# Attention in a hybrid trunk: the two key heads of a head tile issued as a pair on TensorE

## The chip, the cores and the metric

The kernel runs on one core of one Trainium2 chip. The metric is the device time of one execution in microseconds (us), the median of several runs.

## What is computed

Two trunk layers over 256 latent tokens, with 256 context tokens that go through the same weights, width 1024, in fp32. Each layer has a token mixer of three parallel groups (attention, RWKV-7 scan, Hyena long convolution), an output projection, and a channel mixer: a dense SwiGLU in layer 0, a SwiGLU over 8 experts in layer 1. The attention group has 8 query heads of 64 and 2 key heads; latent queries read latent and context keys, context queries read context keys alone:

```python
def gqa_attend(q, k, v):
    s = jnp.einsum('bqgrd,bkgd->bgrqk', q, k, ...) * (HEAD_DIM ** -0.5)
    p = jax.nn.softmax(s, axis=-1).astype(v.dtype)
    return jnp.einsum('bgrqk,bkgd->bqgrd', p, v)
# in each layer, beside the RWKV and Hyena groups:
k_all = jnp.concatenate([kl, kc], 1)    # latent queries: 512 keys
out_lat = gqa_attend(ql, k_all, v_all)
out_ctx = gqa_attend(qc, kc, vc)        # context queries: 256 keys; layer 0 alone
o = jnp.concatenate([att, rwkv, hyena], -1) @ w_out
```

## The kernel before

The program is written in parts (input projection, preparation of the scan, scan, attention, Hyena, output projection, channel mixer), each for one layer and one stream (LAT, CTX). A tile scheduler fixes the order on each engine when the kernel is built: it takes the instruction that is ready by its own estimate, with the program's order as priority. Each engine then works its list off in that order, so an instruction that waits holds up everything behind it on its engine.

`attend` is called three times: for the context tokens of layer 0 (at about 222 to 290 us of the profiled execution), for the latent tokens of layer 0 (about 345 to 461 us) and for those of layer 1 (about 1150 to 1281 us). Other parts lie between its instructions: the RWKV scan, whose states `rS` follow each other as a chain and whose outputs are `rY`, the scan's readout (`ryT`, `rg`), and projections (`u`). A stretch of an attend after the scan's last `rY` is called a tail below: 433 to 461 us and 1239 to 1281 us.

An attend runs over 4 head tiles. A head tile is 128 partitions: head i of key head 0 on partitions 0 to 63, head i of key head 1 on 64 to 127. The queries stand in two tiles of 128 (`qt`). One step is one key head and one query tile, so there are 4 steps in a head tile and 16 in an attend. A step does these: scores `aS` (64 contraction rows, so half of the array's rows; 512 keys, or 256 for the context) on TensorE into one of two PSUM banks of tag "a"; the row maximum and its scaling on VectorE; exp with its sum on ScalarE, giving P (`aP`); transposes of P's 128x128 blocks on TensorE into the only PSUM bank of tag "t" (`aPT`); one copy of that bank by ScalarE into SBUF; and the outputs `ao` (64 output columns, half of the array's columns, 128 queries to a matmul) into a bank of tag "g". After 4 steps `azb` spreads the reciprocal sums over the partitions (through tag "t" too), and two VectorE and ScalarE steps write the head tile's result into `oTa`, which the output projection reads. The loads of that projection's weights go into buffers (`wraw`) that are taken in turn.

```python
BANKS = {"g": 3, "w0": 1, "w1": 1, "a": 2, "t": 1}
```

In a trace a matmul of fp32 data stands as two records, so `x2` there is one score matmul and `x4` two outputs.

Of the kernel before, what the change touches and what calls it, by code (L numbers as in the profile page):

```python
# [15 lines left out]
def feature_tiles():  # L16
    """Columns of w_in per 128-wide tile, -1 for padding."""
# [45 lines left out]
NLAST = 512  # of the first group, kept throughout  # L63
# [8 lines left out]
def constants():  # L72
# [11 lines left out]
    # x -> (-x1, x0) on pairs: out[m] = sum_k perm[k, m] x[k]  # L84
# [14 lines left out]
    ang = np.concatenate([row[:, None] * inv, col[:, None] * inv], -1).astype(np.float64)  # [L, 32]  # L99
# [6 lines left out]
    S = np.sin(th)  # [t, k]  # L106
    S[:, 0] = (-1.0) ** k  # column k = 0 holds the Nyquist term
    put("C", C.reshape(2, 128, 256).transpose(1, 0, 2))
    # forward: lhsT [t, k]; inverse: lhsT [k, t] -> S transposed
# [17 lines left out]
    a, b = (p % 32)[:, None], np.arange(32)[None]  # row s, column t  # L127
    # per direction: (A, B, -A, B) masks; A strict, B inclusive
# [3 lines left out]
    # token order: ltri[p, tt, q] = 1 where token tt*128+p precedes q within the tile  # L132
# [5 lines left out]
    # within a chunk, from its first (second) half to the other one  # L138
# [5 lines left out]
def layout(i):  # L144
    """Device arrays from the inputs: layout only."""
# [9 lines left out]
    aw = g("ada_w").reshape(2, 8, 128, 3, 4, 2, 256)  # l, k, p, r, j, h, n  # L155
    A["adaw"] = np.ascontiguousarray(aw.transpose(0, 3, 5, 1, 2, 4, 6))  # l, r, h, k, p, j, n
# [12 lines left out]
    A["win"] = np.ascontiguousarray(wp.reshape(2, 8, 128, 20, 128).transpose(0, 3, 2, 1, 4))  # l, tile, p, k, 128  # L169
    wo = g("w_out")[:, mix_rows()]  # L170
    A["wout"] = np.ascontiguousarray(wo.reshape(2, 4, 2, 128, 2, 512).transpose(0, 4, 1, 3, 2, 5))  # l, half, kh, p, k, n

    def w13(w1, w3):  # [..., 1024, 2816] -> [..., 11, kh, p, k, (w1 256 | w3 256)]
        e = w1.shape[0]
        u = np.stack([w1, w3], 1).reshape(e, 2, 4, 2, 128, 11, 256)  # e, m, kh, k, p, b, n
        return np.ascontiguousarray(u.transpose(0, 5, 2, 4, 3, 1, 6)).reshape(e, 11, 4, 128, 2, 512)

    def w2(w):  # [e, 2816, 1024] -> [e, half, 22, p, 512]
        e = w.shape[0]
        u = w.reshape(e, 11, 2, 128, 2, 512)  # L180
        return np.ascontiguousarray(u.transpose(0, 4, 1, 3, 2, 5))  # e, half, 11, p, 2, 512
# [6 lines left out]
    A["rows"] = np.stack([g("ln1_g"), g("ln1_b"), g("ln2_g"), g("ln2_b")], 1)  # l, 4, 1024  # L188
    pr = np.zeros((2, 128, NPRM), np.float32)

    def pp(name, a, col=0, r0=0):  # a: [2, rows]
        pr[:, r0:r0 + a.shape[1], PRM[name] + col] = a

    mu = g("rwkv_mu")  # [2, 2, 864]
# [64 lines left out]
class Trunk:  # L259
# [4 lines left out]
    def lasting(s, n):  # L264
        """n words per partition that are kept throughout."""
# [4 lines left out]
    def k(s, shape, name, dt=F32):  # L270
        """A tile. All of the pool's are of 4 KB per partition: up to 1 (2) KB, four (two) of a name share
        one; up to 512 bytes, the slots of a small lasting ring are used in turn."""
# [24 lines left out]
    def fresh(s, *names):  # L297
        """The next small tiles of these names do not share one with the past ones."""
        for n in names:
            s.packs.pop((n, s.w), None)  # L300
# [12 lines left out]
    def split(s, src, hi, lo, eng="a"):  # L313
        """hi + lo == src; both fit a float32r pass exactly."""
# [3 lines left out]
    def mm3(s, out, a, b, start, stop, **kw):  # L318
        """out += a.T @ b from (hi, lo) pairs: three float32r passes."""
# [5 lines left out]
    def rsqrt(s, x, n, eps, name):  # L325
        """x[:, :n] -> 1 / sqrt(x + eps): an estimate from the exponent, then Newton steps to float32."""
# [10 lines left out]
    def raw(s, src):  # L337
        """The next 4 KB per partition of the weight stream."""
# [4 lines left out]
        if s.w == "m" and s.loads % 16 == 0:  # some through another queue  # L343
# [1400 lines left out]
```

## Time and profile before

| | |
|---|---|
| time, median of 3 runs | 2166.26 us (2155.64 to 2171.59) |
| span of the profiled execution | 2151.5 us |
| TensorE (PE) busy | 2061.4 us (96%) |
| VectorE (DVE) busy | 1650.1 us (77%) |
| ScalarE (ACT) busy | 1117.6 us (52%) |

The profile comes from one execution; its span lies 14.8 us below the median and 4.1 us below the fastest run shown. PE is the matmul stream and PEld the loading of its weights, which overlaps it. PEclk is the clock that TensorE was granted, as a share of full speed.

### The profile page before, as it was taken

The page shows a single profiled execution, that of the slowest core. Times are in us where ns is not written, and L with a number is a line of the kernel's source. Part 1 is how long each engine was busy: PE and PEld are TensorE (multiplying, and loading weights), DVE is VectorE, ACT ScalarE, POOL GpSimd, SP SyncE. Part 2 cuts the span into 40 slices and gives each one's busy share as a digit, 9 for nine tenths or more (in the row PEclk, how much of TensorE's full clock was granted, in tenths as well). Part 3 has the DMA queues.
Part 4 walks back from the last instruction along what each step waited for, and adds up shares of the span by engine and source line. Part 5 has one row for each costly group of instructions (what it writes and reads, how often), then busy time and mean ns, then how long its engine had stood idle before and what let it go on. Part 6 is the DMA issues. An engine that isn't in the chain of part 4 may idle for free. (4 is left out here: it accounts for less than half of the span.)

```text
span 2151.5 us, 35770 instructions
## 1 busy us (share of the span) xinstructions
PE 2061.4 (96%) x13674; PEld 1684.2 (78%) x13674; DVE 1650.1 (77%) x3026; ACT 1117.6 (52%) x1639; POOL 111.3 (5%) x87
## 2 busy tenths in 40 slices
PE   8999999999999999989798998999999999999996
PEld 2878777678878898887487777788888888888885
DVE  6897777459754685776887448799899989998997
ACT  3532544242332344443244232787787877778773
POOL 0012001100000000010111100000000000000000
PEclk9999999999999999999899978899999999999998
DMA  8522332336686545323211018699999999999992
GB/s 292 191 74 98 138 129 90 114 115 230 247 335 244 196 177 196 138 88 113 104 60 33 31 56 335 218 319 362 363 334 368 354 344 350 361 358 345 360 356 107
DMA packets 147852, 469.15 MB, mean 218 GB/s; under 512 B 31636, under 2 KB 33972, under 8 KB 147672
## 3 DMA queue, kind: packets, MB, share of 16 engines
q1 hardware_dynamic: 123512, 446.27, 56.8%
q0 software_dynamic: 4816, 17.36, 2.2%
q10 hardware_dynamic: 19344, 3.15, 0.8%
q8 instruction: 109, 1.79, 0.3%
q14 instruction: 71, 0.58, 0.1%
HBM read 464.56 MB, written 2.16 MB: 217 GB/s over the span
## 5 line engine op out<-in xcount | busy, mean ns | idle before, releaser
L316 DVE TENSOR_TENSOR wlo<-wraw,whi 128x1024 fp32r<-128x1024 f32 x748 | 888.0, 1222 | 96.2 <-ACT whi L315 61.7
L315 ACT CAST whi<-wraw 128x1024 fp32r<-128x1024 f32 x748 | 751.7, 1049 | 143.6 <-DMA wraw<-in_fw_dram 40.6
L321 PE MATMUL ab<-whi,m_x 128*128 128x512 f32 x704 | 281.6, 400 | 0.0
L323 PE MATMUL ab<-whi,m_x 128*128 128x512 f32 x704 | 275.6, 391 | 0.0
L322 PE MATMUL ab<-wlo,m_x 128*128 128x512 f32 x704 | 275.0, 391 | 0.0
L321 PE MATMUL ab<-hp,whi 128*128 128x256 f32 x704 | 204.8, 292 | 2.6 <-ACT hp L315 2.0
L323 PE MATMUL ab<-hp,wlo 128*128 128x256 f32 x704 | 201.7, 287 | 1.8 <-DVE wlo L316 1.8
L322 PE MATMUL ab<-hp,whi 128*128 128x256 f32 x704 | 201.7, 287 | 1.3 <-DVE hp L316 1.1
L323 PEld LDWEIGHTS ab<-whi,m_x 128*128 128x128 f32 x704 | 132.1, 188 | 28.3
L321 PE MATMUL u<-hp,whi 128*128 128x256 f32 x512 | 150.2, 297 | 4.1 <-ACT hp L315 3.0
L322 PEld LDWEIGHTS ab<-wlo,m_x 128*128 128x128 f32 x704 | 132.5, 188 | 25.5 <-DVE wlo L316 0.2
L321 PEld LDWEIGHTS ab<-whi,m_x 128*128 128x128 f32 x704 | 132.2, 188 | 25.1
L321 PEld LDWEIGHTS ab<-hp,whi 128*128 128x128 f32 x704 | 135.9, 194 | 18.3 <-issue 11.0
L323 PE MATMUL u<-hp,wlo 128*128 128x256 f32 x512 | 147.9, 291 | 1.2 <-DVE wlo L316 1.1
L322 PE MATMUL u<-hp,whi 128*128 128x256 f32 x512 | 148.1, 292 | 0.0
L323 PEld LDWEIGHTS ab<-hp,wlo 128*128 128x128 f32 x704 | 136.1, 194 | 5.3 <-DVE wlo L316 2.9
L322 PEld LDWEIGHTS ab<-hp,whi 128*128 128x128 f32 x704 | 136.5, 194 | 2.1 <-DVE hp L316 2.0
L321 PE MATMUL mo<-whi,ffg 128*128 128x512 f32 x352 | 137.8, 392 | 0.0
L323 PE MATMUL mo<-whi,ffg 128*128 128x512 f32 x352 | 137.1, 390 | 0.0
L322 PE MATMUL mo<-wlo,ffg 128*128 128x512 f32 x352 | 137.0, 389 | 0.0
L957 POOL TENSOR_TENSOR rBD<-rAT,cst 128x1024 f32<-128x1024 f32 x28 | 67.5, 2418 | 932.8 <-DVE rTm L995 509.9
L321 PEld LDWEIGHTS u<-hp,whi 128*128 128x128 f32 x512 | 98.4, 194 | 15.9 <-issue 6.5
(395 smaller groups left out, 3610.3 us busy)
## 6 DMA issues: line engine op xcount, KB each, us to landing
wraw<-in_mw_dram SPq DMA_DIRECT2D x495, 512.0 KB, 5.6
wraw<-in_fw_dram SPq DMA_DIRECT2D x132, 512.0 KB, 5.2
wraw<-in_adaw_dram SPq DMA_DIRECT2D x96, 512.0 KB, 5.1
wraw<-in_win_dram SPq DMA_DIRECT2D x64, 512.0 KB, 5.7
wraw<-in_mw_dram POOLq DMA_DIRECT2D x33, 512.0 KB, 6.8
wraw<-in_wout_dram SPq DMA_DIRECT2D x24, 512.0 KB, 3.6
lngb<-in_rows_dram SPq DMA_DIRECT2D x12, 512.0 KB, 6.3
x<-in_xs_dram SPq DMA_DIRECT2D x8, 512.0 KB, 6.0
```

Of the source, the lines that this page charges most:

```text
L315: i = (s.nc.scalar.copy if eng == "a" else s.nc.vector.tensor_copy)(hi, src)
L316: return i, s.nc.vector.tensor_sub(lo, src, hi.bitcast(F32))
L321: mm(out, a[0], b[0], start=start, stop=False, **kw)
L322: mm(out, a[0], b[1], start=False, stop=False, **kw)
L323: mm(out, a[1], b[0], start=False, stop=stop, **kw)
L957: i = nc.gpsimd.tensor_mul(x.rearrange("p u (j t) -> p u j t", j=4), bc(ATu[:, :, m, None, :], [128, 8, 4, 32]), bc(mask.rearrange("p (j t ...
```

## The change

A step becomes one query tile with both key heads, so there are 2 steps in a head tile. Both score matmuls are issued one behind the other, ahead of other work that is ready, on rows 0 to 63 and 64 to 127 of the array and into both "a" banks; the first of them is put behind the last exp of the step before. The two transposed blocks go through the one "t" bank in turn, and the second is copied out by VectorE instead of ScalarE. The copies are kept for both query tiles, and the outputs come once in a head tile, at its end: for each block of keys one matmul for each key head, on columns 0 to 63 and 64 to 127, with all 256 queries. Each attend has 8 such steps. Line numbers behind this function are 12 higher in the changed kernel. The rest of the diff takes comments out and is not shown.

```diff
     def attend(s, l, g, oT):
         nc = s.nc
+        mm = nc.tensor.matmul
         ns = 2 if g["st"] == LAT else 1
-        nk = 256 * ns
+        nk, n = 256 * ns, 2 * ns
         q, qrs = g["q"], g["qrs"]
         keys = s.akv[l][:, 0, :ns].rearrange("p a b -> p (a b)")
         vals = s.akv[l][:, 1, :ns].rearrange("p a b -> p (a b)")
+        half, read = [slice(0, 64), slice(64, 128)], None
         for i in range(4):
-            op = s.bank("g", "ao")
+            T = [s.k([128, n, 256], "aPT") for _ in range(2)]
             zs = s.k([128, 2, 2], "az")
-            for g in range(2):
-                r0 = 64 * g
-                for qt in range(2):
-                    S = s.bank("a", "aS")[:, :nk]
-                    nc.tensor.matmul(S, q[r0:r0 + 64, i, 128 * qt:128 * qt + 128], keys[r0:r0 + 64, :], start=True,
-                                     stop=True)
-                    rs = qrs[i][:, 2 * qt + g:2 * qt + g + 1]
+            for qt in range(2):
+                qs = slice(128 * qt, 128 * qt + 128)
+                S = [s.bank("a", "aS")[:, :nk] for _ in range(2)]
+                with s.tc.high_priority():
+                    for h in range(2):
+                        m = mm(S[h], q[half[h], i, qs], keys[half[h], :], start=True, stop=True)
+                        if h == 0 and read is not None:
+                            s.order(m, read)
+                P = []
+                for h in range(2):
+                    rs = qrs[i][:, 2 * qt + h:2 * qt + h + 1]
                     m = s.k([128, 1], "am")
-                    nc.vector.tensor_reduce(m, S, axis=AX.X, op=OP.max)
+                    nc.vector.tensor_reduce(m, S[h], axis=AX.X, op=OP.max)
                     nc.vector.tensor_scalar(m, m, rs, -1.0, op0=OP.mult, op1=OP.mult)
-                    P = s.k([128, nk], "aP")
-                    nc.scalar.activation(P, S, AF.Exp, bias=m, scale=rs, accum_out=zs[:, qt, g:g + 1])
-                    pt = s.bank("t", "aPT")[:, :nk]
-                    for k in range(nk // 128):
-                        nc.tensor.transpose(pt[:, 128 * k:128 * k + 128], P[:, 128 * k:128 * k + 128], s.c("ident"))
-                    T = s.k([128, nk], "aPT")
-                    nc.scalar.copy(T, pt)
-                    for k in range(nk // 128):
-                        nc.tensor.matmul(op[r0:r0 + 64, 128 * qt:128 * qt + 128], vals[:, 128 * k + r0:128 * k + r0 + 64],
-                                         T[:, 128 * k:128 * k + 128], start=k == 0, stop=k == nk // 128 - 1)
-                    yield
+                    P.append(s.k([128, nk], "aP"))
+                    read = nc.scalar.activation(P[h], S[h], AF.Exp, bias=m, scale=rs, accum_out=zs[:, qt, h:h + 1])
+                for h in range(2):
+                    pt = s.bank("t", "aPT")[:, :nk].rearrange("p (k q) -> p k q", k=n)
+                    for k in range(n):
+                        nc.tensor.transpose(pt[:, k, :], P[h][:, 128 * k:128 * k + 128], s.c("ident"))
+                    done = (nc.scalar.copy if h == 0 else nc.vector.tensor_copy)(T[h][:, :, qs], pt)
+                yield
+            op = s.bank("g", "ao")[:, :256]
+            with s.tc.high_priority():
+                for k in range(n):
+                    for h in range(2):
+                        m = mm(op[half[h], :], vals[:, 128 * k + 64 * h:128 * k + 64 * h + 64], T[h][:, k, :],
+                               start=k == 0, stop=k == n - 1)
+                        if h == k == 0:
+                            s.order(m, done)
             nc.vector.reciprocal(zs, zs)
             b = s.bank("t", "azb")[:, :256]
             for qt in range(2):
                 s.spread(b[:, 128 * qt:128 * qt + 128], zs[:, qt])
             f, zb = s.k([128, 256], "mx"), s.k([128, 256], "mx")
             nc.scalar.copy(zb, b)
-            nc.vector.tensor_mul(f, op[:, :256], zb)
+            nc.vector.tensor_mul(f, op, zb)
             s.split(f, *oT[i])
         s.fresh("mx", "aP", "aPT")
```

TensorE's list in the tail of layer 1's attend before, where `aS` is scores, `aPT` transposes, `ao` outputs, `azb` the spread sums and `ryT` the scan's readout (a row's x4 counts equal instructions in a row):

```order
L770 MATMUL aS<-akv,aq 128x512 x2
L784 MATMUL ao<-aPT,akv 64x128 x4
L780 MATMUL aPT<-keep,aP 128x128 x4
L784 MATMUL ao<-aPT,akv 64x128 x4
L702 MATMUL azb<-keep 64x128 x4
L770 MATMUL aS<-akv,aq 128x512
L1181 MATMUL ryT<-keep,rvt 128x128 x4
L780 MATMUL aPT<-keep,aP 128x128 x4
L770 MATMUL aS<-akv,aq 128x512
```

and in the same tail after the change, where `Xc` and `Xs` belong to the Hyena part:

```order
L788 MATMUL aPT<-keep,aP 128x128 x4
L774 MATMUL aS<-akv,aq 128x512 x2
L788 MATMUL aPT<-keep,aP 128x128 x8
L795 MATMUL ao<-aPT,akv 64x256 x2
L774 MATMUL aS<-akv,aq 128x512 x2
L795 MATMUL ao<-aPT,akv 64x256 x6
L702 MATMUL azb<-keep 64x128
L1193 MATMUL ryT<-keep,rvt 128x128 x4
L702 MATMUL azb<-keep 64x128 x3
L788 MATMUL aPT<-keep,aP 128x128 x8
L642 MATMUL Xc<-hvxt,cst_67 128x256
L788 MATMUL aPT<-keep,aP 128x128 x4
L642 MATMUL Xc<-hvxt,cst_67 128x256
```

Before, four transposes and four outputs took turns, with scores and pieces of the readout between; now up to 8 transposes stand in a row, the score pair stands ahead of the outputs of the head tile before, and Hyena's `Xc` has come in between blocks of transposes.

TensorE's list where the chain of scan states `rS` of layer 1's latent tokens runs, before (`rMx` is the matrix that a link multiplies with):

```order
L770 MATMUL aS<-akv,aq 128x512
L1077 MATMUL rS<-rS_11581,rMx_11519 128x64 x2
L784 MATMUL ao<-aPT,akv 64x128 x4
L702 MATMUL azb<-keep 64x128 x4
L770 MATMUL aS<-akv,aq 128x512
L1077 MATMUL rS<-rS_11581,rMx_11518 128x64 x2
L780 MATMUL aPT<-keep,aP 128x128 x4
L770 MATMUL aS<-akv,aq 128x512
L1077 MATMUL rS<-rS_11581,rMx_11518 128x64 x2
```

and after:

```order
L795 MATMUL ao<-aPT,akv 64x256
L1089 MATMUL rS<-rS_11533,rMx_11471 128x64
L774 MATMUL aS<-akv,aq 128x512 x2
L795 MATMUL ao<-aPT,akv 64x256 x7
L1089 MATMUL rS<-rS_11533,rMx_11471 128x64
L702 MATMUL azb<-keep 64x128 x4
L1089 MATMUL rS<-rS_11533,rMx_11470 128x64 x2
L788 MATMUL aPT<-keep,aP 128x128 x4
L1089 MATMUL rS<-rS_11533,rMx_11470 128x64 x2
```

Before, one score matmul or four transposes or four outputs stood between two links; now a score pair with seven outputs stands in one gap, and the other gaps hold four transposes or four of `azb`.

## Rows read from the trace of the kernel before

**Rows 1.** page: span; engine: busy us, share, instructions

```profile
span 2151.5 us, 35770 instructions
...
PE 2061.4 (96%) x13674; PEld 1684.2 (78%) x13674; DVE 1650.1 (77%) x3026; ACT 1117.6 (52%) x1639; POOL 111.3 (5%) x87
```

**Rows 2.** stretch, length, busy of PE PEld DVE ACT POOL, clock, DMA share, GB/s

```profile
222.00:290.00 68.00, 67.73 (x520) 52.26 (x513) 47.96 (x134) 36.25 (x90) 0.00 (x0) 1.00 0.33 118
345.00:433.00 88.00, 86.18 (x750) 63.08 (x750) 45.80 (x131) 29.54 (x63) 13.66 (x8) 1.00 0.26 91
433.00:461.00 28.00, 28.00 (x179) 18.66 (x179) 13.71 (x42) 10.41 (x24) 0.00 (x0) 0.82 0.17 58
1180.00:1239.00 59.00, 58.72 (x529) 43.27 (x528) 25.69 (x67) 15.16 (x33) 10.32 (x4) 0.94 0.09 28
1239.00:1281.00 42.00, 40.65 (x197) 28.45 (x197) 16.40 (x47) 14.66 (x33) 0.00 (x0) 0.67 0.00 1
...
1500.00:1700.00 200.00, 200.00 (x924) 165.32 (x923) 185.17 (x208) 155.79 (x196) 4.22 (x8) 1.00 0.96 351
```

**Rows 3.** timeline, layer 0, latent tail; start, us, engine, line

```profile
446.29 0.66 PE L780 MATMUL aPT<-keep,aP 128*128 128x128 f32 x4
...
446.88 1.12 PE L770 MATMUL aS<-akv,aq 64*128 64x512 f32 x2
446.99 0.58 ACT L782 COPY aPT<-aPT 128x512 f32<-128x512 f32 x1 [1.74 <-PE aPT L780]
...
447.93 1.09 PE L784 MATMUL ao<-aPT,akv 128*64 128x128 f32 x8
...
448.95 0.66 PE L780 MATMUL aPT<-keep,aP 128*128 128x128 f32 x4
```

**Rows 4.** timeline, layer 0, context attend

```profile
264.53 0.70 PE L770 MATMUL aS<-akv,aq 64*128 64x256 f32 x2
...
265.15 0.44 PE L702 MATMUL rkb<-keep 128*64 128x128 f32 x4
...
267.94 0.65 PE L784 MATMUL ao<-aPT,akv 128*64 128x128 f32 x4
...
268.52 0.44 PE L780 MATMUL aPT<-keep,aP 128*128 128x128 f32 x2
```

**Rows 5.** timeline, layer 1, latent scan

```profile
1177.99 2.00 PE L1051 MATMUL rM<-rbx,rPQ 128*64 128x256 f32 x16
...
1179.77 0.59 PE L1059 MATMUL rN<-rvx,rkbt 128*64 128x256 f32 x2
...
1195.29 0.56 PE L1077 MATMUL rS<-rS,rMx 128*128 128x64 f32 x4
...
1196.58 0.66 PE L1077 MATMUL rS<-rS,rMx 128*128 128x64 f32 x4
```

**Rows 6.** TensorE and its granted clock by stretch

```profile
1231.00:1234.00 3.00, 3.00 (x21) 0.50 0.00 0
...
1245.00:1271.00 26.00, 24.65 (x83) 0.50 0.00 0
1272.00:1282.00 10.00, 10.00 (x85) 1.00 0.01 2
435.60:445.70 10.10, 10.10 (x51) 0.50 0.16 53
```

**Rows 7.** groups of the softmax and the copy, by shape

```profile
L777 ACT ACTIVATE aP<-aS,keep 128x512 f32<-128x512 f32 x32 | 24.8, 780 | 7.6 <-PE rN L1059 3.8 <-DVE keep L775 2.3 <-PE rN L1061 1.5
...
L774 DVE TENSOR_REDUCE keep<-aS 128x1 f32<-128x512 f32 x32 | 22.0, 689 | 26.8 <-PE aS L770 26.8
...
L777 ACT ACTIVATION_READ_ACCUMULATOR aP<-aS,keep 128x1 f32 x48 | 9.6, 200 | 0.0
L775 DVE TENSOR_SCALAR keep<-keep 128x1 f32<-128x1 f32 x48 | 9.6, 207 | 0.2
```

**Rows 8.** SP's waits around layer 1's attention

```profile
SPq L347 <- DVE oTa L316: 72.9, 1, 72.9
```

## The prediction

> **What bounds the kernel now.** I read the page first: TensorE is busy for 96% of the span [rows 1], so a step that only frees another engine gives little. An average says nothing of a stage, so the next view is the table of stretches around the three attends [rows 2]. In the context attend TensorE is busy 67.73 of 68 us, in the latent attend of layer 0 86.18 of 88 before the scan's last output and 28.00 of 28 in the tail, in layer 1 58.72 of 59 and 40.65 of 42. No other engine comes near: VectorE has 25.69 of the 59 and 16.40 of the 42. So TensorE's own list, in order, sets the time there, and microseconds taken out of it come off the end unless the list then starts to wait. The expert stage is full on TensorE too (200.00 of 200) [rows 2]; it has nothing of this change in it, and what starts earlier by some time ends earlier by it. Its weights do not stand against that: the loads of the output projection wait 72.9 us for VectorE's last attention output [rows 8], so they move ahead with the attention.
>
> The last view is the clock. It is not the same in all these stretches: 1.00 in the context attend, 0.82 and 0.67 in the two tails [rows 2], and the finer stretches show where: 0.50, the lower level of 1.2 GHz, in 435.6 to 445.7 and 1245 to 1271, with TensorE busy 10.10 of 10.10 and 24.65 of 26 us, and back to 1.00 (2.4 GHz) from 1272 [rows 6]. What ran there were the half-array matmuls of the attention between transposes and pieces of the readout.
>
> **What a step costs.** A latent step at full clock is read from one turn of the tail: transposes start at 446.29, scores at 446.88, outputs at 447.93, the next transposes at 448.95 [rows 3]. That is 0.59 + 1.05 + 1.02 = 2.66 us, and 10.6 for the 4 steps of a head tile. A context step has scores of 0.62 (264.53 to 265.15) and outputs of 0.58 (267.94 to 268.52) [rows 4].
>
> **Outputs by column halves.** The trace of before has just this shape in the scan: `rM`, 256 columns, on alternating halves of the array's columns, has 16 records from 1177.99 to 1179.77, 1.78 us [rows 5]. A latent head tile after the change has 4 key blocks by 2 heads, 8 matmuls, 16 records: 1.78 for 4 x 1.02 = 4.08, a gain of 2.30. A context head tile has half of it, 0.89 for 4 x 0.58 = 2.32, a gain of 1.43. For the 4 head tiles that is 9.2 in each latent attend, 5.7 in the context's, 24.1 in all.
>
> **Scores by row halves.** No row of before shows two row halves at once. The bounds are nothing (4 x 1.05 as now) and a full overlap (2 x 1.05, a gain of 2.1 in a latent head tile; 2 x 0.62 = 1.24 in a context one). I take the full overlap, since the nearest row is that of the column halves, 1.78 where four times 1.02 stood. With it a latent head tile gains 4.4, the context's 2.67: 17.6 + 17.6 + 10.7 = 45.9 us of TensorE's time in the three attends, with the lower bound 24.1.
>
> For row halves the Trainium skill, "TensorE: Matmul & The Clock Gate", Part 3, gives a measured 3.07 times for four row tiles at once; by it, as an estimate, two would come close to twice and the term would be the full overlap. No row here shows it.
>
> **What else moves.** Transposes are the same in number. Half of the copies, 24 in the three attends, go to VectorE; a copy by ScalarE takes 0.58 [rows 3], so 24 are at most 14 us over stretches in which VectorE has over 100 us free [rows 2]: nothing. Its price if that cover were gone is the 14. The two blocks of a pair share the single "t" bank: transposes start at 446.29, the copy at 446.99 takes 0.58 [rows 3], so with the hand-over a turn is about 1.4 us, an estimate. Before, scores and outputs (2.07) filled it; now up to 8 transposes stand in a row, and 4 turns of a head tile are 5.6 us, in which its transposes take 4 x 0.59 = 2.4. The rest must be filled by the score pairs, the outputs, the readout, Hyena's `Xc`. Last, the pair needs both "a" banks and so waits for both exps of the step before; behind it on TensorE's list is queued all that follows, the scan's links among it.
>
> **The sum,** against the span of 2151.5. Context attend: half of 10.7 is taken, 5, as its short steps leave least to fill a wait with. Latent attend of layer 0: some two of the four head tiles fall before the last scan output, 8.8 by the sum. The states are a chain there, whose next link follows after 1.29 us (1195.29 to 1196.58) [rows 5], and attention fills its gaps; less of it ends the stretch sooner only as far as the chain lets it. I take half, 4.4. Its tail: two head tiles, 8.8 at full clock and up to 10.7 at 0.82; I take 7, for the turns of the "t" bank. Layer 1 before 1239: the same 4.4. Its tail of 42 us: two head tiles of 10.6 - 4.4 = 6.2, 7 with a turn that waits, and 3 for `azb` and the readout make 17 at full clock, a gain of 25; if it all stays at 0.50 it is 34, a gain of 8. I take 15, between them: both halves of the array work at once now, which speaks for the higher level, but the projections `u`, which stood among the steps, are now behind them and fill less. Sum: 5 + 4.4 + 7 + 4.4 + 15 = 35.8. The span would be 2115.7; the median of the runs shown lies 14.8 above the span, and from it the forecast is 2166.3 - 35.8 = **2131** (rounded up).
>
> Its own bounds: 10 more in the last tail, 5.7 more in the context attend and 4.4 more beside layer 0's chain make 56 and 2110. With 8 in the last tail, nothing in the context attend and 2 less in the first tail it is 22 and 2144.
>
> **Rivals.** (1) The row halves run one after the other. For it: no row shows them together. The sum shrinks as 24.1 to 45.9, to 19, and the time is 2147.
>
> (2) The chain of states and the turns of the bank hide it. Then the stretches before the last scan outputs give nothing, nor the context attend. A head tile in a tail is 5.6 of turns, 2.1 of score pairs and 1.8 of outputs one behind the other, 9.5 for 10.6: a gain of 2 in layer 0's tail, and 12 in layer 1's, where 2 x 9.5 + 3 = 22 make 20 in place of 25 at full clock and I discount as above (15 of 25). Gain 14, time 2152. Against it: tails have readout and Hyena work to stand between the turns.
>
> The Trainium skill, "TensorEngine Tiling (Array Packing)", PSUM Bottleneck, says that packing speeds up the matmuls but not the emptying of PSUM, and wants both ScalarE and VectorE for it, as here; this rule is on the side of that rival, whose price above comes from the rows.
>
> (3) The clock stays low. If TensorE now waits in the tails, both could run at 0.50 to their end: 8 in layer 1's tail, nothing in layer 0's, where 8.8 saved goes into more time at half clock, and 2 elsewhere. Gain 10, time 2156. Against it: at 0.50 the engine was already busy 10.10 of 10.10 us [rows 6], so idling was not what preceded the fall there.
>
> The Trainium skill, "TensorE: Matmul & The Clock Gate", HAM oscillation, says that gaps in which TensorE idles bring the clock down; rows 6 show a low clock with no gap, so the trace bears the rule out little, and that rival gets a small chance.
>
> (4) Slower: TensorE waits at each score pair. From the end of a pair to the release of both banks there are, at least, two row maxima of 0.689 (the exp of the first beside the second), a scaling of 0.207, an exp of 0.780 and its sum of 0.200 [rows 7], 2.57 us. With the list in order and nothing of value between, 16 latent steps wait 41 us; the context's 8 steps, with half the keys, some 15 (an estimate). That is 56 less 45.9, 10 slower; the scan's links behind the pair wait with it, and if the gaps double the time at half clock in one tail, another 12: 2188 to 2190. It decides if on average less than 2.57 - 45.9/24 = 0.7 us of other work stands between a pair and the next. Against it: four transposes alone are 0.59 [rows 3], and the lists after the change show links, outputs and `azb` between the pairs as well.
>
> (5) The change doesn't do what it says only in that the pairs are not started together; that is (1).
>
> **How the numbers follow.** The forecast has 0.50, (1) 0.10, (2) 0.18, (3) 0.06, (4) 0.12, and better than its own bounds (under 2110) 0.04. The range of 2108 to 2165 takes in the forecast and rivals (1) to (3), and leaves out (4) and half of the last case, 0.14. A measurement of this kernel can tell about 1% from no change, 21.7 us: faster is under 2144.6, slower over 2187.9. Faster holds the forecast but for its edge (0.48), the better case (0.04) and the luckiest part of (1) (0.03): 0.55. Slower holds the greater part of (4), 0.09; the rest, 0.36, is within 1%.
>
> **What would show it.** Outputs: 16 records of `ao` in about 1.8 us, not 3 to 4. Scores: both heads' records start together and a pair takes about 1.05 us; 2.1 means (1). Turns: transposes follow the ScalarE or VectorE copy of the block before, with TensorE idle before them; under 0.3 us a turn is the forecast, 0.8 is (2). Clock: the granted clock of layer 1's tail, 0.67 before, over 0.8 for the forecast. Waits: TensorE idle before the score pairs for ScalarE's exps, together under 5 us; over 30 is (4). The expert stage should keep its length and only start earlier. I would be wrong if that stage does not move with the attention's end, or if the order of the list, which the change moves everywhere in these attends, makes a wait far from the attention longer.

## The result, and the profile after

The changed kernel takes 2132.36 us (median of 4 runs, 2126.04 to 2134.47), the kernel before 2168.93 (4 runs, 2155.64 to 2178.42): ratio 0.9857, 95% interval 0.9817 to 0.9897. A second comparison with more runs (e1 below) gave 2132.89 against 2160.02 and 0.9846 (0.9806 to 0.9886). The forecast was 2131.

The profiled execution of after has a span of 2132.7 us, 18.8 less than that of before [rows 1], while the medians differ by 37 in the first comparison and by 27 in the second. A difference of single executions is not enough here, because the granted clock differs from run to run. For the comparisons below each run's span is therefore cut in two: **work** = span times the run's mean granted clock, which is what the span would be at full clock, and **lost** = the rest. Over 20 runs of before and 6 of after on one chip the work falls from 2080.1 to 2059.9 us (by 20.2, interval 16.5 to 23.9) and the lost time from 80.1 to 69.9 (by 10.1, interval 4.3 to 15.9). So about two thirds of the gain are less work and one third is clock. The split is rough by a microsecond or two: over 67 runs of before, one microsecond more of lost time goes with 0.83 us more of span, not with 1. All figures of work and lost time leave out three slow runs of before, which were over 1.5% above the fastest beside e9 to e11.

The page of after, span and TensorE:

```profile
span 2132.7 us, 35433 instructions
...
PE 2033.8 (95%) x13514; PEld 1656.6 (78%) x13514; DVE 1659.7 (78%) x3050; ACT 1105.6 (52%) x1615; POOL 111.1 (5%) x87
```

TensorE is busy 27.6 us less, VectorE 9.6 more: the copies. The stretches of after (columns as in [rows 2]); they are cut where the same events fall, the scan's last outputs `rY` and the end of the attends:

```profile
225.00:295.00 70.00, 69.33 (x484) 49.71 (x484) 47.40 (x136) 33.77 (x81) 0.00 (x0) 0.88 0.24 86
225.00:238.00 13.00, 13.00 (x47) 10.19 (x47) 6.31 (x17) 4.70 (x11) 0.00 (x0) 0.50 0.01 1
345.00:441.00 96.00, 93.89 (x793) 66.91 (x793) 51.44 (x152) 31.98 (x70) 13.14 (x8) 0.91 0.29 94
409.60:426.00 16.40, 16.36 (x88) 10.91 (x90) 3.69 (x12) 2.74 (x7) 0.00 (x0) 0.50 0.44 160
441.00:459.00 18.00, 16.00 (x112) 9.82 (x112) 12.73 (x37) 6.35 (x15) 0.00 (x0) 1.00 0.21 66
1180.00:1234.00 54.00, 52.63 (x491) 36.94 (x488) 28.28 (x71) 12.40 (x28) 9.32 (x4) 0.94 0.08 30
1234.00:1260.00 26.00, 23.13 (x142) 15.38 (x142) 18.11 (x51) 11.11 (x25) 0.00 (x0) 0.87 0.30 102
1236.00:1242.00 6.00, 6.00 (x18) 3.31 (x18) 4.48 (x10) 2.26 (x5) 0.00 (x0) 0.50 0.45 162
...
1500.00:1700.00 200.00, 200.00 (x924) 165.30 (x923) 185.15 (x208) 155.88 (x195) 4.24 (x8) 1.00 0.96 354
```

The reader is to see three things beside [rows 2]. The tail of layer 1's attention takes 26 us where it took 42, that of layer 0 takes 18 for 28. The clock in layer 1's tail is 0.87 where it was 0.67, in layer 0's 1.00 where it was 0.82; but 13 us at half clock stand now in the context attend, which had none, and 16 us beside layer 0's scan. The expert stage has the same records and the same busy time, so it only starts earlier.

How far after is ahead of before at each place can be read from the starts of the VectorE and ScalarE instructions that both kernels have, matched one by one; their median shift in a stretch of 5 to 50 us is given here. It is -1.4 us at 220, +6.1 at 295, -3.0 at 465, -2.8 at 1150, and -19.3 from 1400 to the end. Set beside the clock of each stretch (length times one minus the clock), that splits the three attends:

| | forecast | shift | of it clock | the rest: work |
|---|---|---|---|---|
| context attend | -5 | +7.5 | +8.4 (70 x 0.12, none before) | -0.9 |
| layer 0, latent | -11.4 | -9.1 | +3.6 (96 x 0.09 - 28 x 0.18) | -12.7 |
| layer 1, latent | -19.4 | -16.5 | -10.8 (54 x 0.06 + 26 x 0.13 - 59 x 0.06 - 42 x 0.33) | -5.7 |

The work adds to -19.3, and many runs say -20.2. The clock's share of this pair of executions is +1.2, that of many runs -10: which of two single executions is luckier in its clock is what the medians average out.

**Do the halves run at once?** The tail of layer 1's attention after, TensorE's timeline (`aS` scores, `aPT` transposes, `ao` outputs):

```profile
1239.20 2.08 PE L774 MATMUL aS<-akv,aq 64*128 64x512 f32 x4
1241.21 1.56 PE L788 MATMUL aPT<-keep,aP 128*128 128x128 f32 x8
1243.00 0.65 PE L795 MATMUL ao<-aPT,akv 128*64 128x256 f32 x2 [0.23 <-ACT aPT L789]
1244.37 0.65 PE L795 MATMUL ao<-aPT,akv 128*64 128x256 f32 x2 [0.72 <-DVE aPT L789]
1244.94 1.13 PE L774 MATMUL aS<-akv,aq 64*128 64x512 f32 x4
1246.00 1.52 PE L795 MATMUL ao<-aPT,akv 128*64 128x256 f32 x12
1247.35 0.38 PE L702 MATMUL azb<-keep 128*64 128x128 f32 x2
```

At full clock a score pair takes 1.06 us (1244.94 to 1246.00), as long as one score matmul did (1.05) [rows 3]; at half clock, in the stretch that ends at 1242, it takes 2.01. Twelve output records take 1.35 (1246.00 to 1247.35), 0.11 each, as `rM` had [rows 5]. So both overlaps exist. But a head tile's outputs come here in pieces of 2, 2 and 12, and a piece of 2 takes 0.55 at full clock on average, not 0.22; and TensorE waits 0.23 and 0.72 for copies.

Of the 15 latent pairs that are neighbours on TensorE's list, nine take 1.00 to 1.13 us at full clock and six 1.28 to 1.81. In four of these six the second score starts when its bank is free, as here:

```profile
1191.52 0.78 ACT L784 ACTIVATE aP<-aS,keep 128x512 f32<-128x512 f32 x1 [1.21 <-PE aPT L788]
1192.20 0.19 ACT L784 ACTIVATION_READ_ACCUMULATOR aP<-aS,keep 128x1 f32 x1
1192.29 0.77 ACT L784 ACTIVATE aP<-aS,keep 128x512 f32<-128x512 f32 x1
1192.44 1.88 PE L774 MATMUL aS<-akv,aq 64*128 64x512 f32 x4
1192.95 0.20 ACT L784 ACTIVATION_READ_ACCUMULATOR aP<-aS,keep 128x1 f32 x1
1193.20 0.29 PEld L774 LDWEIGHTS aS<-akv,aq 64*128 64x128 f32 x2 [0.47 <-ACT aP L784]
```

The first score starts 0.05 us after the first exp's sum has ended (1192.39), the second, with its weights, 0.05 us after the second's (1193.15). So a pair does not start behind the last exp of the step before, as the section on the change and the prediction have it: each score waits for its own bank. The line `s.order` in the diff puts an instruction behind another in the scheduler's plan and asks for no wait between the engines (it names the dependency NoSync).

In the context attend the scheduler has taken 6 of the 8 pairs apart, in spite of their priority:

```profile
240.04 0.70 PE L774 MATMUL aS<-akv,aq 64*128 64x256 f32 x2
240.67 0.38 PE L321 MATMUL u<-hp,whi 128*128 128x256 f32 x1
240.98 0.70 PE L774 MATMUL aS<-akv,aq 64*128 64x256 f32 x2
241.61 0.39 PE L322 MATMUL u<-hp,whi 128*128 128x256 f32 x1
```

Each of these scores takes 0.63 alone, as before [rows 4].

TensorE's waits from 285 to 475 us in after (who waited for whom; total, times, longest):

```profile
PE aS L774 <- DVE keep L713: 1.7, 1, 1.7
PE akb L702 <- DVE keep L727: 1.5, 1, 1.5
PE aPT L788 <- ACT aP L784: 1.5, 1, 1.5
PE rPQ L1031 <- ACT whi L315: 0.7, 1, 0.7
PE rtr L986 <- ACT rkbt L989: 0.6, 1, 0.6
PE aS L774 <- ACT aP L784: 0.6, 1, 0.6
```

TensorE stands idle before a score pair for an exp for 0.6 us in the whole attend, in one place; in the other two attends no such wait reaches 0.2 us.

### The profile page after: what moved, and what is told of

Same layout as the page of the kernel before. It is cut to its first block, busy times and chain, and to the rows that moved or that the text cites. A ratio compares the mean times of both kernels' runs of the same rounds, so it can differ in the third digit from the quotient of the medians.

```text
span 2132.7 us, 35433 instructions
## 1 busy us (share of the span) xinstructions
PE 2033.8 (95%) x13514; PEld 1656.6 (78%) x13514; DVE 1659.7 (78%) x3050; ACT 1105.6 (52%) x1615; POOL 111.1 (5%) x87
## 5 line engine op out<-in xcount | busy, mean ns | idle before, releaser
L321 PEld LDWEIGHTS ab<-whi,m_x 128*128 128x128 f32 x704 | 132.2, 188 | 25.1
```

The source lines that it names most:

```text
L321: mm(out, a[0], b[0], start=start, stop=False, **kw)
```

## Experiments

All runs are against runs of the kernel before on the same chip, in four groups: e1 to e4, e5 to e8, e9 to e11, e12. The two columns of change are differences of means of work and of lost time to before, with 95% intervals; before itself had a work of 2080.1, 2076.4, 2078.8 and 2077.2 us in the four groups. A difference between two rows has an interval of some 5 us within a group, and across groups the 3.7 by which before itself moves come in.

| | runs | median us | ratio to before (interval) | work | lost |
|---|---|---|---|---|---|
| e1 the change again | 6 | 2132.89 | 0.9846 (0.9806 to 0.9886) | -20.2 ± 3.7 | -10.1 ± 5.8 |
| e2 scores on one row half | 8 | 2144.04 | 0.9911 (0.9877 to 0.9945) | -13.9 ± 3.7 | -4.5 ± 6.4 |
| e3 outputs by halves in turn | 7 | 2142.75 | 0.9903 (0.9868 to 0.9938) | -13.4 ± 3.8 | -6.7 ± 5.5 |
| e4 both edits | 12 | 2154.87 | 0.9969 (0.9942 to 0.9995) | -1.4 ± 3.1 | -5.2 ± 4.3 |
| e6 copies on ScalarE | 6 | 2142.53 | 0.9900 (0.9856 to 0.9944) | -5.0 ± 4.4 | -13.9 ± 6.9 |
| e7 no forced order | 12 | 2147.63 | 0.9957 (0.9920 to 0.9993) | -8.5 ± 2.8 | -1.8 ± 7.6 |
| e8 context attend as before | 6 | 2133.38 | 0.9859 (0.9817 to 0.9901) | -12.3 ± 4.0 | -16.0 ± 5.2 |
| e9 two "t" banks | 6 | 2142.51 | 0.9896 (0.9848 to 0.9944) | -10.2 ± 4.1 | -11.0 ± 6.0 |
| e10 copies on VectorE | 11 | 2145.16 | 0.9920 (0.9888 to 0.9952) | -7.0 ± 3.4 | -9.2 ± 5.4 |
| e11 before, copies on both | 12 | 2161.69 | 0.9991 (0.9958 to 1.0025) | 0.0 ± 3.3 | -1.3 ± 6.3 |
| e12 forced order in latent only | 6 | 2129.62 | 0.9815 (0.9768 to 0.9862) | -19.0 ± 4.3 | -20.3 ± 7.1 |

**e1, the change again.** No edit.

> The changed kernel unaltered, a second time, as the base for the other three on the same chip and for the clock. Its first profile had a span of 2132.7 us at a mean clock of 0.965, that of before 2151.5 at 0.967, so the span times the clock fell by 22 us where the medians fell by 37. If freed TensorE time is what pays (theory), span times clock is again 2055 to 2062, about 22 under that of before (2080), and the rest of the difference between medians is the clock of single runs. If the change itself gives back clock (rival), its clock is higher than that of the runs of before on the same chip by 0.005 or more.

Work 2059.9, inside the theory's 2055 to 2062. The clock, 0.967 against 0.963 of before on the same chip, is higher by 0.004, just under the 0.005 that was named for the rival, and its interval leaves out zero: so both hold, 20 us of work and 10 of clock.

**e2, both scores of a pair on rows 0 to 63.**

```diff
-                        m = mm(S[h], q[half[h], i, qs], keys[half[h], :], start=True, stop=True)
+                        m = mm(S[h], q[half[0], i, qs], keys[half[0], :], start=True, stop=True)
```

> Both score matmuls of a pair use rows 0 to 63 (so the second head's scores are computed from the first head's data, a changed part of the computation); TensorE's list is the same. Theory: the row halves overlap in the changed kernel, 1.06 us for a pair at full clock; here a pair takes 2.1, so 16 latent pairs cost up to 1.05 each, some of it lost where the second matmul waited for an exp anyway: 10 to 16 us slower than e1 in span times clock. Rival (the gain came from the new order of the list and from fewer, larger pieces): within 4 us of e1.

6.3 us of work more than e1 (interval 1.6 to 11.0), under the 10 to 16 of the theory and over the 4 of the rival, so that the size is uncertain. TensorE's list in the three attends is that of after, record by record, so this is the cleanest of the edits. The trace of e2 shows the price of one pair:

```profile
1232.16 1.98 PE L774 MATMUL aS<-akv,aq 64*128 64x512 f32 x4
1234.07 1.94 PE L795 MATMUL ao<-aPT,akv 128*64 128x256 f32 x14
```

1.91 us (1232.16 to 1234.07) where two halves take 1.06: the row halves overlap in full, and 0.85 is what a pair wins over two scores back to back. The 1.05 of the forecast had in it the start of a run, which the second of two neighbours saves. 16 latent pairs of that size would be 13.6 us, not 16.8. Counted over all records (the way of counting is told in the next section), e2's scores take 40.1 us for 29.6 in after, since not all pairs overlapped in full there, and of these 10.5 us 6.3 show in the work.

**e3, the column halves in another order.**

```diff
-                        m = mm(op[half[h], :], ..., start=k == 0, stop=k == n - 1)
+                        m = mm(op[half[2 * k // n], :], ..., start=h == 0 and 2 * k % n == 0,
+                               stop=h == 1 and 2 * (k + 1) % n == 0)
```

> The outputs of the first half of the key blocks go to columns 0 to 63, those of the second half to 64 to 127, for both heads (the sums are of the wrong terms, a changed part of the computation), so neighbours no longer stand on different column halves but at one place in eight. Theory: 16 records of a latent head tile take 16 x 0.27 = 4.3 us instead of 1.8, 2.2 more with the one place that still overlaps, over 8 latent head tiles 18, and 4 in the context attend: 14 to 22 us slower than e1 in span times clock. Rival (order and waits pay): within 4 us of e1.

6.8 us of work more than e1, half of the least that was expected. The edit took away less overlap than it was meant to: of the fourteen records shown next, four start 0.01 to 0.06 us after another one, so some neighbours still stand on different halves. (Which halves they are, and whether the scheduler changed their order, the trace does not name.) Fourteen records in e3's layer 1:

```profile
1231.55 2.43 PE L795 MATMUL ao<-aPT,akv 128*64 128x256 f32 x14
1233.91 0.32 PE L1124 MATMUL rY<-rS,rkr 64*32 64x64 f32 x8
```

and in after at the same place:

```profile
1225.90 1.94 PE L795 MATMUL ao<-aPT,akv 128*64 128x256 f32 x14
1227.78 0.32 PE L1124 MATMUL rY<-rS,rkr 64*32 64x64 f32 x8
```

2.36 us for 1.88: 0.5 a head tile, where 2.2 was expected. Counted over all records its outputs take 27.2 us for 23.3, so 3.9 of overlap were taken away, not 22. And between 150 and 600 us TensorE's list differs from that of after in 697 records, so that the 6.8 us of work can't all be put down to the overlap.

**e4, both edits.**

> Both edits of e2 and e3: the steps, copies and order of the change with hardly an overlap on the array. Theory: the sum of the two, 24 to 38 us slower than e1, so as slow as before or some us slower. Rival: within 6 us of e1, faster than before by 1%.

18.8 us of work more than e1, a little under the 24 to 38, and 1.4 ± 3.1 from before: the change's steps, its forced order and its copies on two engines, with some of the overlap taken out (scores and outputs take 67.4 us of TensorE's time, 52.9 in after, 78.0 before), have no work to show for themselves. The two edits together cost more than e2 and e3 singly (18.8 against 13.1), within what their intervals allow. But the list of e4 is that of e3, not that of after: it differs in the same 697 records between 150 and 600 us, and in 8 around layer 1's attention. So the two attends are to be read apart. The table sets, against e1, the TensorE time of scores and outputs beside the length at full clock of the stretch around each latent attend (300 to 480 and 1150 to 1450 us, between the same VectorE and ScalarE instructions); one trace each, and two traces of the changed kernel differ by 1.6 and 0.6 us in the stretches.

| against e1 | layer 0: TensorE time | stretch | layer 1: TensorE time | stretch |
|---|---|---|---|---|
| e2 | +4.4 | +4.1 | +5.0 | +4.0 |
| e3 | +0.1 | +4.1 | +2.0 | +1.4 |
| e4 | +5.7 | +12.6 | +7.2 | +6.3 |

Where the list is the same (e2 in both layers, e3 and e4 in layer 1 but for those 8 records), the stretch grows by 0.7 to 0.9 of the overlap that was taken away, and layer 1's stretch, 7.1 us shorter than before in e1, is only 0.8 shorter in e4. So in layer 1 the gain in work is the overlap. In layer 0 another list adds 4 to 7 us in e3 and e4, and how much of their loss is overlap is not shown there.

**e5, before again, one profile.**

> The kernel before, unaltered, for a second trace of it. If where the clock falls is set by the program (theory), its stretches at 0.50 lie where the first trace had them: 27 us in the tail of layer 1's attention, 31 us behind it, 10 us in the tail of layer 0's, none in the context attend. If it is chance (rival), they lie elsewhere, and the 10 us of clock that the medians differ by, beyond the 20 us of work, can't be ascribed to the change.

Stretches at 0.50 in the second trace of before:

```profile
427.50:447.50 20.00, 20.00 (x109) 0.50 0.09 28
1243.00:1263.00 20.00, 19.33 (x81) 0.50 0.00 1
```

In layer 1's tail the clock falls again, for 20 us (27 in the first trace), around the start of layer 0's tail for 20 (from 9 us before it; 10 in the first trace, all in the tail), behind layer 1's attention for 31 as in the first, and again not in the context attend. A stretch of 10 us at the start of layer 0's latent attend (335.0 to 345.3) is new; there the first trace has 3.4. So most places recur with the program, and their lengths differ from run to run.

**e6, all copies on ScalarE.**

```diff
-                    done = (nc.scalar.copy if h == 0 else nc.vector.tensor_copy)(T[h][:, :, qs], pt)
+                    done = nc.scalar.copy(T[h][:, :, qs], pt)
```

> All copies of transposed blocks on ScalarE, none on VectorE. Theory: the copies lie beside other work, within 3 us of e1 in span times clock. Rival (turns of the one bank set the pace in the tails, and two engines take turns better): 5 us or more slower than e1.

The theory falls: of the 20 us of work only 5 are left. But the rival's place is not where the loss is. Matched to e1 instruction by instruction, e6 goes from 1 to 3 us ahead at 300 to 10.8 behind at 450 and is 9.8 behind at the end: nearly all of it arises in layer 0's latent attend, and in layer 1's, whose tail has the same turns, none (2.6 us at full clock). TensorE's waits in e6 from 285 to 475 us:

```profile
PE akb L702 <- DVE keep L727: 4.4, 1, 4.4
PE u L321 <- ACT rkbt L989: 3.4, 1, 3.4
PE rS L1089 <- DVE rS L1091: 2.8, 4, 1.7
PE ryT L1193 <- DVE keep L799: 2.7, 1, 2.7
PE aPT L788 <- ACT aP L784: 2.2, 1, 2.2
```

These are 15.5 us, where the first six of after were 6.6, and none of the five is for a copy or the "t" bank. Other engines for the copies gave another list (over 1300 of TensorE's 13514 records stand elsewhere than in after), and in that list TensorE stands before the keys' norm, a projection, the states and the readout. The overlaps are there: scores and outputs take 50.3 us, less than the 52.9 of after.

**e7, no priority and no order for pairs and outputs.**

```diff
-                with s.tc.high_priority():
+                with contextlib.nullcontext():
                     for h in range(2):
                         ...
-                        if h == 0 and read is not None:
+                        if False:
...
-            with s.tc.high_priority():
+            with contextlib.nullcontext():
...
-                        if h == k == 0:
+                        if False:
```

> The same steps and instructions, but the scheduler is free to place score pairs and outputs: no priority and no order behind the exp or the copy. In TensorE's list the two scores of a pair then stand apart in 14 of 16 latent steps and adjacent in 6 of 8 context steps. Theory (overlap pays): the latent pairs lose most of the 6.6 and 5.7 us that they freed, so 5 to 10 us slower than e1 in span times clock. Rival 4 of the prediction in a small form (the forced pair waits for both exps): equal or faster than e1.

11.7 us less work saved than in e1 (8.0 if the works of e7 and e1 are compared without their runs of before), about the 5 to 10 of the theory; here too the list is another one, in over 1500 records. A latent score of e7, at half clock, stands alone and takes what a pair of after took there (2.01):

```profile
1212.61 2.07 PE L774 MATMUL aS<-akv,aq 64*128 64x512 f32 x2
1214.61 1.12 PE L795 MATMUL ao<-aPT,akv 128*64 128x256 f32 x4
```

And no gain of the clock is shown (-1.8 ± 7.6). Its trace has a low stretch in layer 1's attention as long as that of before (27 us), in another place, with TensorE busy throughout:

```profile
1203.00:1229.00 26.00, 26.00 (x131) 0.50 0.17 61
```

**e8, the context attend as before.** The old function stands beside the new one, under another name:

```diff
-        s.go(s.attend(0, g, oT[CTX]))
+        s.go(s.attend1(0, g, oT[CTX]))
```

> The context attend as before, the two latent ones as changed. By the traces the change frees only 3 us of TensorE time in the context attend (6 of 8 score pairs are taken apart by the scheduler), and 17 us at half clock lie there that the trace of before lacks, 8.6 us lost. Theory: 1 to 4 us slower than e1 in span times clock; if the clock's fall is tied to the context attend, its lost time is 5 to 9 us less than that of e1 and it is 2 to 6 us faster in all. Rival: the lost time is the same as in e1, and it is 1 to 4 us slower.

The median is that of e1 (2133.38 to 2132.89). The work is 7.9 more than e1's, over the 1 to 4 expected, but with an interval of some 5 us and with layer 0's list changed too; the lost time of both lies within their intervals (-16.0 ± 5.2, -10.1 ± 5.8). The trace has a low stretch before and at the start of the old context attend too:

```profile
219.50:229.70 10.20, 10.20 (x46) 0.50 0.54 220
```

So, as far as one trace shows it, the fall of the clock there isn't tied to the new context attend.

**e9, two "t" banks.**

```diff
-    BANKS = {"g": 3, "w0": 1, "w1": 1, "a": 2, "t": 1}
+    BANKS = {"g": 2, "w0": 1, "w1": 1, "a": 2, "t": 2}
```

> The changed kernel with two banks of tag t and two of tag g (before: one and three). Theory: turns of the one bank cost little, since TensorE's idle time in the attends is 4 to 7 us each; within 5 us of e1 in span times clock. Rival 2 of the prediction (the turns of the bank hold it up): 5 to 12 us faster, most of it in the two tails.

10.0 us more work than e1: neither. Matched to e1, e9 falls behind by 5 us at 100 and by 20 at 450, where the "g" banks also serve other parts. Around layer 1's attend (1150 to 1450) it gains 7 us on e1, but that is clock: it has 3 us at half clock there before 1300 where e1 has 20, and at full clock its stretch is 3.5 us longer. So no gain of a second "t" bank is shown, and one edit that also takes a "g" bank away can't price the two apart.

**e10, all copies on VectorE.**

```diff
-                    done = (nc.scalar.copy if h == 0 else nc.vector.tensor_copy)(T[h][:, :, qs], pt)
+                    done = nc.vector.tensor_copy(T[h][:, :, qs], pt)
```

> All copies of transposed blocks on VectorE. e6, all on ScalarE, was 12 us slower than e1 in span times clock, all of it in the latent attend of layer 0 and none in layer 1's. If two engines in turn are what pays (theory), this one is slower than e1 by 5 to 15 us too, and in both latent attends. If e6's loss came from another order of the list in layer 0 (rival), this one is within 4 us of e1 in layer 1, and layer 0 follows its own list.

13.2 us more work than e1. Matched to e1 it goes from 9 us ahead at 300 to 7.2 behind at 450, and from 5.1 to 6.5 behind over layer 1's attend: again layer 0, hardly layer 1, which is the rival's answer. But here the copies are waited for; TensorE's waits from 285 to 475 us:

```profile
PE rPQ L1031 <- DVE rTT L1020: 6.5, 1, 6.5
PE ao L795 <- DVE aPT L789: 4.3, 4, 1.8
PE aS L774 <- DVE aPT L789: 4.3, 2, 3.1
```

8.6 us wait for VectorE's copies, 6.5 for VectorE's part of the scan's preparation. So beside layer 0's scan VectorE has no room for all of them.

**e11, before with its copies on two engines.**

```diff
-                    nc.scalar.copy(T, pt)
+                    (nc.scalar.copy if g == 0 else nc.vector.tensor_copy)(T, pt)
```

> The kernel before with one edit: the copies of key head 1 go to VectorE, the steps unchanged. Theory (the overlaps pay): within 4 us of the kernel before in span times clock. Rival (the copies on two engines are a good part of the gain): 8 us or more faster than before.

0.0 ± 3.3 of work: the copies alone bring nothing.

**e12, forced order in the latent attends alone.**

```diff
-                with s.tc.high_priority():
+                with s.tc.high_priority() if ns == 2 else contextlib.nullcontext():
...
-                        if h == 0 and read is not None:
+                        if h == 0 and ns == 2 and read is not None:
```

and the same two edits at the outputs.

> The changed kernel, but the scheduler is free in the context attend alone (no priority, no order there); the latent attends keep theirs. In e7 the free context attend had 6 of 8 score pairs adjacent, 5.5 us of scores in place of 8.7, and took 48.5 us of full-clock time from the scan's last output to its own last output where e1 took 53.0. Theory (adjacent pairs overlap, and TensorE's time there comes off the end): 3 to 5 us faster than e1 in span times clock, the lost clock as in e1, so 2125 to 2131 us. Rival: layer 0's list behind it changes too and waits more, as in e6, and eats it: within 2 us of e1 or slower.

The context pairs are now adjacent in 7 of 8 steps and overlap:

```profile
254.94 0.70 PE L774 MATMUL aS<-akv,aq 64*128 64x256 f32 x4
255.58 0.44 PE L788 MATMUL aPT<-keep,aP 128*128 128x128 f32 x2
```

0.64 us for a pair. The stretch from the scan's last output to the context attend's own last one shrank by 3.9 us at full clock (49.1 for 53.0), yet the work as a whole is -19.0 against e1's -20.2: the list of layer 0 behind it changed too, and that stretch (300 to 480 us) grew by 7.7 us at full clock, as the rival had it. Against its own runs of before e12 has the best ratio of all, 0.9815, but its interval overlaps that of e1 (0.9806 to 0.9886), so it is not shown to be better than the change.

## Why the prediction came out right, step by step

**The time** is right: 2131 forecast, 2132.4 and 2132.9 measured. The sum behind it is right in kind and off in its terms: it had 35.8 us, most of it freed TensorE time, and there were 20 of work and 10 of clock. The hit to within 2 us is luck in part: the 35.8 were taken from 2166.3, the median of three runs of before, and 20 runs of it have 2160.0.

**What bounds the kernel.** Right. The expert stage kept its length and moved ahead with the attention's end (-19.3 us at its start and at its end).

**Scores by row halves.** The choice of the full overlap is right (1.06 a pair, 1.91 in e2), rival (1) is out. The size is not. Counted over all records of the first traces (each to the next one of TensorE or its own end, times the granted clock), the scores of the three attends take 8.5, 16.6 and 16.6 us before and 8.7, 10.9 and 10.0 after. So the latent attends free 5.7 and 6.6 where 8.4 each were forecast, since in some pairs the second score comes only when its bank is free (1.81 us for the pair shown above), and the context attend frees nothing where 5 were forecast, since its pairs are taken apart. I took "issued one behind the other" from the code; what the diff asks for is a priority, and the order on TensorE's list in the context attend was there to be read.

**Outputs by column halves.** The price of a full run was right (0.11 a record), the term was not: 7.5, 14.5 and 14.3 us before, 4.2, 9.9 and 9.2 after, so 4.6 and 5.1 freed where 9.2 each were forecast, and 3.3 for 5.7. Before was too dear in the sum (the 1.02 of one turn stood for all, 4.08 x 4 = 16.3 against 14.4), and after too cheap (pieces such as 2, 2 and 12 records, 9.5 against 4 x 1.78 = 7.1). All in all 25 us of TensorE time were freed, not 45.9: the lower bound of the forecast's own range, 24.1, for another reason. Of these 25 about 20 came off the end.

That share is no constant. Freed TensorE time, counted in this way, and the work that came off are 25.1 and 20.2 us in e1 and 14.6 and 13.9 in e2, both with the list of the change; but 27.7 and 5.0 in e6, 28.9 and 7.0 in e10, 30.2 and 19.0 in e12, with other lists. The forecast's condition, that freed time comes off "unless the list then starts to wait", is what decides: the freed time was a ceiling, and what each list lost elsewhere took 1 to 23 us of it.

The Trainium skill, "TensorE: Matmul & The Clock Gate", Part 3, names 3.07 times for four row tiles; the trace agrees in kind with 1.06 us for two against 1.91 one behind the other, 1.8 times.

**The copies,** costed at nothing with a price of 14 if their cover were gone. The cover is there on each engine for half of them: all on VectorE cost 13.2 us of work and TensorE then waits 8.6 for them; all on ScalarE cost 15.2, with no wait for a copy but another list. As a part alone they are worth nothing (e11). So the edit belongs to the gain, by its cover or by the list that comes with it, which these runs don't tell apart; the forecast's "nothing" holds only for the change as a whole.

**The turns of the "t" bank,** rival (2). In layer 1's tail TensorE is idle 2.9 of 26 us after, where it was idle 1.4 of 42 [rows 2]: some of it is these waits (0.23 and 0.72 before outputs), so they exist and are small. The sign named for it, TensorE idle before transposes for the copy of the block before, comes to 0.5 us in the context attend, 0.2 in layer 1 and less in layer 0, so the turns are not the main limit. The tails gave 10 and 16 us where the forecast had 7 and 15; but at full clock that is 5.0 (28 x 0.82 - 18) and 5.5 (42 x 0.67 - 26 x 0.87), between the 2.2 of two head tiles in rival (2) and the 8.8 of the forecast. What two "t" banks would bring is open (e9).

**The clock.** In layer 1's tail the forecast of 15 was a mean of 25 and 8, for an open level of the clock. The granted clock went from 0.67 to 0.87, over the 0.8 that I named as the mark, and of the 16 us of that tail 10.5 are clock (42 x 0.33 - 26 x 0.13). Rival (3) is out. Over many runs the lost time falls by 9 to 20 us in the kernels with both overlaps (e1, e6, e8, e9, e10, e12), by 4 to 7 in those with one or both taken away (e2, e3, e4), and by 1 to 2 where the latent scores stand alone (e7, e11), with intervals of 4 to 8. That the overlap is the cause is not shown, and the sum's reason for the higher level, both halves at work at once, is not borne out: in layer 1's attend the half clock cost 17.1 us in both traces of before and 6.8 and 10.2 in the two of the change, but only 3.4 in e4, with most of that attend's overlap taken out. In the three attends together it cost 22.2 and 32.5 us in the two traces of before, 23.8 and 27.2 in those of the change, so single traces do not show where the 10 us of the many runs come off. What lifts the clock stays open.

The Trainium skill, "TensorE: Matmul & The Clock Gate", HAM oscillation, puts a low clock down to gaps in TensorE's work. Here the gaps of layer 1's tail grew (1.4 to 2.9 us) while its clock rose, and in e7 it was at 0.50 with TensorE busy 26.00 of 26 us: in these stretches the trace speaks against idling as the cause.

**Slower, rival (4).** Out: TensorE stood idle for 0.6 us before a score pair, for an exp, in the whole latent attend of layer 0. Enough other work stood between the pairs, which was the point from which it was to decide; and the pair does not wait as a whole: each score waits for its own bank, and the first runs while the second bank is still being read. What the forced order does is to make latent pairs neighbours, and without it (e7) about half of the gain in work is gone.

## What to carry to other kernels

Price a pair of half-array matmuls from a run of neighbours, not from one turn of a loop: the first of a run has a start in it that the second saves, and a run cut into pieces pays it again. Before forecasting an overlap, read on the engine's list whether the two instructions are neighbours at each place; a priority in the code does not make them so. Take freed time as a ceiling, and compare variants whose list is the same, because another list took 4 to 9 us in layer 0 here (e3, e4, e6, e12). Where the granted clock moves by itself, take span times clock and the lost rest apart over many runs, because one pair of executions can put ten microseconds on the wrong side.

## What the runs showed of the hardware that was not expected

Two matmuls of 64 contraction rows on the two row halves, into two banks, start together and end as one (1.06 us at full clock, 2.01 at half clock). Two on the same half, one behind the other, take 1.91, less than twice 1.05. The granted clock falls to 0.50 in much the same parts of the program again and again (two traces of before: 27 and 20 us in layer 1's tail, 10 and 20 around layer 0's), with TensorE busy 24.65 of 26 us (before) and 26.00 of 26 (e7) in such stretches, and the mean clock over many runs lies 0.000 (e11) to 0.009 (e12) above that of before, according to the kernel.
